# A hybrid decoder layer on one core: k and the second half's x transposed by VectorE blocks and transfers, two sample products run in pairs

## The chip, the cores and the metric

The kernel runs on one core of a Trainium2 chip. The core has TensorE (PE, with its weight loads shown as PEld), VectorE (DVE), ScalarE (ACT), GpSimd (POOL) and SyncE (SP), which issues all DMAs of this kernel on one queue in program order. The metric is the device time of one launch in microseconds (us); lower is better.

## The reference, cut to what matters

One layer (depth 1) is applied to a prompt of 2048 tokens and to a sample group of 8 sequences with 4 tokens each, with the same weights; the width is 1024 and there are 8 heads of 128.

```python
h = _layernorm(x) * (1 + scale) + shift          # scale, shift from silu(c) @ w_ada
p = h @ w_in                                     # 9232 columns
u_a, v_a, z_a, qkv, z_b, b_raw, a_raw, ga, gb = split(p)
y_a = gelu(u_a) * (tril(w_s) @ layernorm(gelu(v_a)) + b_s) * silu(z_a)   # chunks of 128 tokens
q, k, v = silu(causal depthwise conv of width 4 over qkv)
q, k = l2norm per head; beta = sigmoid(b_raw); g = -exp(a_log) * softplus(a_raw + dt_bias)
# gated delta rule, chunked:  S_t = a_t S_(t-1) + beta_t k_t (v_t - a_t S_(t-1)^T k_t)^T,  o_t = S_t^T q_t
y_b = rmsnorm(o) * silu(z_b)
m = sigmoid(ga) * (y_a @ w_pa) + sigmoid(gb) * (y_b @ w_pb)
x_new = layernorm(ALPHA * x + gate * (m @ w_o))
```

For the sample group the delta rule starts from a given state of 8 sequences x 8 heads x 128 x 128, and the new states are outputs too.

## The kernel before

The prompt is worked on in two halves of 1024 tokens; the sample's 32 tokens ride with the first half. Each half runs the same list of column groups ("groups") of 128 output columns: for each head k, q, v, z_b and (heads 0 to 5) g_a, then g_b, v_a, u_a with z_a, the rest of g_a, then the products with w_pa, w_pb and w_o. A group is computed in column pieces of tokens, `CG`: 384, 384 and 256+32 tokens in the first half, 512 and 512 in the second. Every fp32 operand is split into two fp32r parts, so one piece is 8 x 3 matmuls into one of three PSUM banks (role `mm`), and its "sink" (a generator such as `qkv_sink`) then evacuates the bank.

All activations live transposed (features on partitions, tokens along the row), so whatever needs tokens on partitions is transposed. `k_token` does that for k with TensorE (`tp`, one 128x128 transpose for each chunk of 128 tokens), takes the squares' sums from PSUM on ACT, and writes the scaled k into the buffer `KV`, which `chain` reads. `q_token` transposes q the same way, for the norm alone. `v_token` has another route: `qkv_sink` transposes v in 32x32 blocks on VectorE (`vtrans`), and four DMAs write the blocks to DRAM (`d_v`) in runs of 32 elements so that a fifth DMA reads them back with tokens on partitions. The convolution's working buffers have the role `cp`: there are two, taken for each sink of k, q and v; k and q give theirs back when the product with the tanh has been written to `KQ`, v gives its back after the fourth write to `d_v`.

`gram` of a head needs q and k of a piece and the norm of k (`cc`, made in `k_token`). `inverse` follows `gram`, and `chain` walks the 8 chunks of a half in order. When the last head of the second half is done (`headdone`), the Y buffers take the split weights of v_a (`v_take`), and `v_tokens` multiplies with them. While the first half's later groups run, `h_next` normalizes x of the second half, transposes it by `tp` (8 chunks x 8), applies scale and shift out of PSUM (`affine`) and writes it to `d_h`; `h_tiles` loads it back at the end of the first half and splits it.

`sample_head` does the sample's delta rule for one head: eight products `kx` (64 output columns, 128 columns streamed) accumulate q and k against the eight sequences' states, and two products with `kp` (32 rows contracted, 512 columns streamed) make the update of the states.

The order of instructions on every engine is fixed when the program is built: a list scheduler (`Sched`) takes the steps of all generators, gives each step an assumed duration and lets the step that can start first go next. On the chip the engines follow that order and wait on semaphores.

Of the kernel before, what the change touches and what calls it, by code (L numbers as in the profile page):

```python
# [169 lines left out]
def hybrid_step_kernel(ctx: ExitStack, tc: tile.TileContext, x_prompt, x_sample, state_conv, state_ssm,  # L170
# [53 lines left out]
    def dram(name, n):  # L224
        return dr_pool.tile([1, n], F32, name=name)[:]
# [6 lines left out]
    def role(name, cands):  # L232
        roles[name] = cands
# [8 lines left out]
    def Yc(first, n):  # L242
        return (YO + first * UNIT, xs_units(32, first, n))
# [95 lines left out]
    def SCR(**kw):  # L339
# [18 lines left out]

    d_v = {(half, h, i): dram(f"d_v{half}{h}{i}", n * P)
           for half, ns in enumerate(((384, 384, 256), (512, 512))) for h in range(H) for i, n in enumerate(ns)}  # L360

# [439 lines left out]
    def h_next(c):  # L801

        yield from x_norm(1, c, "hb")
        xb, t0 = S.ev[("xn", 1, c)]
        e = 0.0
        for i in range(2):
            pb = yield ("a", "pt")
            t = t0
            for k in range(4):
                t = yield from tp(Q(pb[0], k * P, P), V(xb[0] + (4 * i + k) * P, P), dep=max(t, pb[2]))  # L810
            fb = yield ("a", "hf")
            tg = max(t, fb[2])
            for k in range(4):
                t = yield from affine(V(fb[0] + k * P, P), Q(pb[0], k * P, P), 4 * i + k, k < 2, tg)
                e = max(e, t)
            S.release(pb, e)
            t = yield from dma(DV(d_h, 4 * i * P * HALF + c * P, [HALF, P], [P * HALF, 4], [1, P]),
                               V(fb[0], [P, 4], [1, P]), dep=e)
            S.release(fb, t)
            S.signal(("hB", c, i), t + 500)  # L820
        S.release(xb, e)

    def h_next_all():
        for c in range(8):
            S.spawn(h_next(c), 2.0)
            if c:
                yield ("w", ("hB", c - 1, 1))

# [7 lines left out]
    def h_tiles(todo, role, after):  # L836
        if after is not None:
            yield ("w", after)
        while todo:
# [6 lines left out]
            for c in range(8):  # L846
                t = max(t, (yield ("w", ("hB", c, k // 4))))
# [339 lines left out]
    def qkv_sink(half, s, h):  # L1187
# [13 lines left out]
        def sink(cgi, pb, t):  # L1201
# [38 lines left out]
            else:  # L1240
# [11 lines left out]
                S.spawn(k_token(half, h, cgi, t) if s == 1 else q_token(half, h, cgi, t), 1)  # L1252
            if ns_:
# [57 lines left out]

    def k_token(half, h, cgi, t):
        me = hd(half, h)
        tk = yield ("w", ("kd", half, h))
        cs = chunks(half, cgi)
        m, c0 = len(cs), cs[0]
        hs = me["hs"][0]
        if "KV" not in me:
            if "KVw" not in me:
                me["KVw"] = True  # L1320
                kv = yield ("a", "KV")
                me["KV"] = kv
                S.signal(("KV", half, h), kv[2])
        ta = yield ("w", ("KV", half, h))
        pb = yield ("a", "pt")
# [14 lines left out]
        S.release(pb, t)  # L1340
# [303 lines left out]
    def sample_head(h):  # L1644
        me = hd(0, h)
        t = 0.0
        for s in range(3):
# [25 lines left out]
        t = yield from pow_(V(o_vf, 1, **k32), V(o_vf, 1, **k32), 1)  # L1673
        kp, vs = x + 64, x + 192
        t = yield from ts(V(kp, P, **k32), Q(pb[0], 0, P, **k32), V(o_kf, 1, **k32), ALU.mult)
        t = yield from ts(V(vs, P, **k32), Q(pb[0], P, P, **k32), V(o_vf, 1, **k32), ALU.mult)
        S.release(pb, t)
        es, npq, am, m2, us = x + 320, x + 352, x + 416, x + 448, x + 480
        t1 = yield from tt(V(es, NS, **k32), V(gr, NS, **k32), V(c_mns, NS, **k32), ALU.add, dep=t1)
# [8 lines left out]
        t = yield from tp(Q(pb[0], 64, NS, **k32), V(npq, NS, **k32))  # L1688
        t = yield from act(V(am, NS, **k32), Q(pb[0], 64, NS, **k32))
# [3 lines left out]
        t = yield from tt(V(us, NS, **k32), V(m2, NS, **k32), Q(pb[0], 128, NS, **k32), ALU.subtract)  # L1693
        S.release(pb, t)
# [10 lines left out]
        t4 = 0.0  # L1705
# [4 lines left out]
        rb = yield ("a", "Rb")  # L1710
        t = yield from stt(V(rb[0], P, **k32), Q(pb[0], 0, P, **k32), V(c_sneg + h, 1, **k32), V(vs, P, **k32),
                           ALU.mult, ALU.add, dep=max(t4, t, rb[2]))
        osb = yield ("a", "Xb")
        q32 = dict(p0=32, np_=32)
        t5 = yield from act(V(osb[0], P, **q32), Q(pb[0], 0, P, **q32), dep=max(t4, osb[2]))
        S.release(pb, max(t, t5))
        pb = yield ("a", "pt")
        t = yield from mm(Q(pb[0], 0, P, **k32), V(us, NS, **k32), V(rb[0], P, **k32), dep=max(t, pb[2]))
        t = yield from act(V(rb[0], P, **k32), Q(pb[0], 0, P, **k32))
        tx = t  # L1720
# [12 lines left out]
        tz = yield ("w", ("zz", 0, h, len(CG[0]) - 1))  # L1733
        ys = x + 448
        t = yield from stt(V(ys, NS), Q(pb[0], 0, NS), V(c_ong, 1), V(me["ZZ"][0] + HALF, NS),
# [7 lines left out]
                           bc(V(egr + 3, [4, 8]).unsqueeze(2), [P, 8, P]), ALU.mult, dep=max(t2, t4))  # L1743
        for i in range(2):
            xe = yield ("a", "kx")
            t1 = yield from tt(V(xe[0], [P, 4], [1, P], **k32), bc(V(rb[0], P, **k32).unsqueeze(1), [NS, 4, P]),
                               bc(V(c_sel + 4 * i, 4, **k32).unsqueeze(2), [NS, 4, P]), ALU.mult, dep=max(tx, xe[2]))
            pb = yield ("a", "pt")
            t = yield from mm(Q(pb[0], 0, 512), V(kp, P, **k32), V(xe[0], 512, **k32), dep=max(t1, pb[2]))
            S.release(xe, t)  # L1750
            a = V(sb0[0] + 512 * i, 512)
            t = yield from tt(a, a, Q(pb[0], 0, 512), ALU.add, dep=max(t, t2))
            S.release(pb, t)
        S.release(rb, t1)
# [561 lines left out]
```

## Time and profile before

| what | value |
|---|---|
| runs | 2719.08, 2723.06, 2724.36 us (median 2723.06) |
| the profiled execution | 2721.62 us, of which the span from the first to the last instruction is 2719.9 us |
| PE / PEld busy | 2676.6 us (98%) / 2351.3 us (86%) |
| DVE / ACT / POOL busy | 1467.0 us (54%) / 1002.8 us (37%) / 557.0 us (20%) |
| mean granted TensorE clock | 0.997 |
| DMA queue | 445402 packets, 269.89 MB, 34.6% of 16 engines' span |

Times in the rows below are in microseconds from the span's start unless a row says ns. An fp32 matmul shows as two records, a transpose or an fp32r matmul as one. A record's duration includes the pipeline's latency, so what one costs is read from start to start.

### The profile page before, as it was taken

The page shows a single profiled execution, that of the slowest core. Times are in us where ns is not written, and L with a number is a line of the kernel's source. Part 1 is how long each engine was busy: PE and PEld are TensorE (multiplying, and loading weights), DVE is VectorE, ACT ScalarE, POOL GpSimd, SP SyncE. Part 2 cuts the span into 40 slices and gives each one's busy share as a digit, 9 for nine tenths or more (in the row PEclk, how much of TensorE's full clock was granted, in tenths as well). Part 3 has the DMA queues.
Part 4 walks back from the last instruction along what each step waited for, and adds up shares of the span by engine and source line. Part 5 has one row for each costly group of instructions (what it writes and reads, how often), then busy time and mean ns, then how long its engine had stood idle before and what let it go on. Part 6 is the DMA issues. An engine that isn't in the chain of part 4 may idle for free.

```text
span 2719.9 us, 44021 instructions
## 1 busy us (share of the span) xinstructions
PE 2676.6 (98%) x16386; PEld 2351.3 (86%) x16386; DVE 1467.0 (54%) x3234; ACT 1002.8 (37%) x2710; POOL 557.0 (20%) x1452
## 2 busy tenths in 40 slices
PE   6999999999999999999999999999999999999998
PEld 3989999999899999999997888888888888888876
DVE  5677667777652353433547666666662323433446
ACT  5544444545343222221224535344542312222120
POOL 2044544324400000000000443433351000000001
PEclk9999999999999999999999999999999999999999
DMA  6232333223463232332433333333332422233332
GB/s 214 68 95 78 90 105 91 72 70 101 141 211 95 64 115 76 94 105 91 140 109 101 96 97 81 85 93 78 84 86 83 125 99 76 72 112 104 108 121 85
DMA packets 445618, 272.70 MB, mean 100 GB/s; under 512 B 141530, under 2 KB 411154, under 8 KB 445403
## 3 DMA queue, kind: packets, MB, share of 16 engines
q1 hardware_dynamic: 445402, 269.89, 34.6%
q8 instruction: 128, 2.10, 0.3%
q14 instruction: 88, 0.71, 0.1%
HBM read 205.70 MB, written 64.10 MB: 99 GB/s over the span
## 4 chain that ended last, share of the span: by engine, by line
PE 95%; DMA 2%; DVE 1%; ACT 1%; issue 0%; SPq 0%; POOL 0%; POOLq 0%; ACTq 0%; DVEq 0%
PE psum L447 90%; PE psum L452 3%; DMA arena<-in_w_o_dram 0%; ACT arena L398 0%; DMA arena<-in_w_in_dram 0%; PE psum L1483 0%; PE psum L1509 0%; PE psum L1520 0%; DVE arena L730 0%; DMA arena<-in_state_ssm_dram 0%; DVE arena L732 0%; PE psum L1489 0%; DVE arena L423 0%; PE psum L650 0%; DMA Y0F<-in_x_prompt_dram 0%
## 5 line engine op out<-in xcount | busy, mean ns | idle before, releaser
L447 PE MATMUL psum<-TX,TWHL 128*128 128x384 f32 (+3 forms) x9296 | 1973.4, 360 | 3.8 <-DVE TX L407 3.4
L447 PEld LDWEIGHTS psum<-TX,TWHL 128*128 128x128 f32 (+1 forms) x9296 | 1554.6, 188 | 164.0 <-issue 10.6
L398 ACT ACTIVATE arena<-psum 128x128 bf16<-128x128 f32 (+10 forms) x920 | 311.8, 348 | 769.9 <-PE psum L447 587.9
L436 POOL TENSOR_TENSOR arena<-arena 128x4 f32<-128x4 f32 (+4 forms) x139 | 120.1, 865 | 1598.3 <-DVE arena L417 1388.7
L423 DVE SCALAR_TENSOR_TENSOR arena<-arena 128x512 f32<-128x512 f32 (+8 forms) x625 | 345.8, 563 | 95.3 <-ACT arena L398 84.9
L410 POOL TENSOR_TENSOR arena<-arena 128x60 f32<-128x60 f32 (+24 forms) x992 | 358.6, 361 | 169.6 <-DMA d_v<-arena 57.5
L407 DVE TENSOR_TENSOR TWHL<-arena,TWHL 128x512 fp32r<-128x512 f32 (+1 forms) x344 | 233.1, 685 | 240.9 <-ACT TWHL L398 238.7
L423 DVE SCALAR_TENSOR_TENSOR arena<-arena,psum 128x128 f32<-128x128 f32 (+3 forms) x342 | 132.2, 403 | 360.3 <-PE psum L447 249.9
L398 ACT ACTIVATE TWHL<-arena 128x512 fp32r<-128x512 f32 x344 | 214.3, 627 | 219.1 <-PE psum L447 103.4
L398 ACT ACTIVATE arena<-arena 128x128 f32<-128x128 f32 (+9 forms) x509 | 229.4, 486 | 118.2 <-DVE arena L423 81.8
L407 DVE TENSOR_TENSOR arena<-arena 128x1024 f32<-128x1024 f32 (+13 forms) x259 | 114.3, 446 | 15.0 <-DMA arena<-in_lnv_g_dram 4.9
L447 PE MATMUL psum<-arena 128*128 128x128 f32 (+8 forms) x524 | 102.3, 293 | 1.2 <-ACT arena L398 1.0
L452 PE MATMUL psum<-arena 128*128 128x128 f32 (+7 forms) x381 | 93.2, 269 | 3.4 <-ACT TX L398 1.5
L423 DVE SCALAR_TENSOR_TENSOR arena<-psum,arena 128x512 f32<-128x512 f32 (+4 forms) x80 | 39.8, 509 | 103.8 <-PE psum L447 103.8
L447 PEld LDWEIGHTS psum<-arena 128*128 128x128 f32 (+5 forms) x524 | 73.7, 162 | 22.9 <-issue 11.2
L1228 POOL COPY arena<-arena 128x3 f32<-128x3 f32 x120 | 34.7, 289 | 267.7 <-ACT arena L398 266.8
L398 ACT ACTIVATE TX<-arena 128x512 fp32r<-128x512 f32 (+2 forms) x84 | 47.3, 587 | 93.6 <-DMA arena<-d_yb 74.2
L398 ACT ACTIVATE Y7F<-psum 32x256 f32<-32x256 f32 (+6 forms) x115 | 46.6, 405 | 86.0 <-PE psum L447 38.4
L398 ACT ACTIVATION_READ_ACCUMULATOR arena<-psum 128x1 f32 x392 | 76.6, 195 | 0.0
L452 PEld LDWEIGHTS psum<-arena 128*128 128x128 f32 (+7 forms) x381 | 49.9, 136 | 23.0 <-issue 11.9
L407 DVE TENSOR_TENSOR TX<-arena,TX 128x512 fp32r<-128x512 f32 (+2 forms) x84 | 52.4, 639 | 26.3 <-ACT TX L398 25.7
L417 DVE TENSOR_SCALAR arena<-arena 128x3 f32<-128x3 f32 (+10 forms) x234 | 47.8, 209 | 34.0 <-ACT arena L398 25.8
(244 smaller groups left out, 2733.6 us busy)
## 6 DMA issues: line engine op xcount, KB each, us to landing
arena<-in_w_in_dram SPq DMA_DIRECT2D x288, 256.0 KB
out_dram<-arena SPq DMA_DIRECT2D x25, 512.0 KB
arena<-in_x_prompt_dram SPq DMA_DIRECT2D x24, 512.0 KB
arena<-d_gc SPq DMA_DIRECT2D x16, 512.0 KB
arena<-d_blk SPq DMA_DIRECT2D x64, 128.0 KB
d_yb<-arena SPq DMA_DIRECT2D x32, 256.0 KB
d_vh<-arena SPq DMA_DIRECT2D x16, 512.0 KB
arena<-d_vh SPq DMA_DIRECT2D x16, 512.0 KB
```

The costliest lines, as they stand in the source:

```text
L398: nc.scalar.activation(out, in_, func, **kw)
L407: nc.vector.tensor_tensor(out=out, in0=a, in1=b, op=op)
L410: nc.gpsimd.tensor_tensor(out=out, in0=a, in1=b, op=op)
L417: nc.vector.tensor_scalar(out=out, in0=a, scalar1=s1, scalar2=s2, op0=op0, **kw)
L423: nc.vector.scalar_tensor_tensor(out=out, in0=a, scalar=s, in1=b, op0=op0, op1=op1)
L436: nc.gpsimd.tensor_tensor(out=out, in0=a, in1=e, op=ALU.pow)
L447: nc.tensor.matmul(out, lhsT, rhs, start=start, stop=stop)
L452: nc.tensor.transpose(out, in_, ident[: in_.shape[0], : in_.shape[0]] if idn is None else idn)
L1228: nc.gpsimd.tensor_copy(V(c_tail + gi, [24, 3]), V(x0 + n0, 3))
```

## The change

- `k_token` no longer uses TensorE. `qkv_sink` transposes k in blocks on VectorE, and a new `tokens` does for k what `v_token` does for v: four writes to a new DRAM buffer `d_k`, one load into `KV`. The squares and the scaling then read `KV`. The `cp` buffer of a k sink is given back after the fourth write.
- `h_next` transposes a whole chunk of x by one VectorE instruction and writes it with four DMAs in runs of 32 elements; scale and shift move to `h_tiles`, where they are applied to a loaded tile of 128x1024.
- In `sample_head` the eight `kx` products go to two column halves of the array in turn, each half accumulating in its own 64 partitions; an ACT copy and a VectorE addition join them. The two `kp` products go to two groups of 32 rows, with copies of `kp` and of the right operand on partitions 32 to 63.

```diff
-    role("hf", [Yc(2, 1), Yc(3, 1), Yc(6, 1), Yc(7, 1)])
+    role("hf", [Yc(2, 2), Yc(6, 2)])
...
     def h_next(c):
         yield from x_norm(1, c, "hb")
-            for k in range(4):
-                t = yield from tp(Q(pb[0], k * P, P), V(xb[0] + (4 * i + k) * P, P), dep=max(t, pb[2]))
...
-                t = yield from affine(V(fb[0] + k * P, P), Q(pb[0], k * P, P), 4 * i + k, k < 2, tg)
...
+        fb = yield ("a", "hf")
+        t = yield from vtrans(V(fb[0], D), V(xb[0], D), dep=max(t, fb[2]))
+        S.release(xb, t)
+        for i in range(4):
+            t = yield from dma(DV(d_h, c * P + 32 * i, [HALF, 32], [32 * HALF, 32], [1, 32]),
+                               V(fb[0], [32, 32], [1, 32], p0=32 * i, np_=32), dep=t)
...
             t = yield from dma(V(b[0], HALF), DV(d_h, k * P * HALF, [HALF, P], [1, HALF]), dep=max(t, b[2]))
+            t = yield from affine(V(b[0], HALF), V(b[0], HALF), k, k % 2 == 0, t)
             t = max(t, (yield ("w", ("Xfree", 1, k))))
...
                 t = yield from stt(dst, V(x0, n0), 1.0, y, ALU.add, ALU.mult, dep=max(t, ta))
-                S.release(xb, t)
                 S.signal(("kq", half, h, s, cgi), t)
+                if s == 1:
+                    t = yield from vtrans(V(x0, n0), dst)
+                    S.spawn(k_token(half, h, cgi, xb, t), 1)
+                else:
+                    S.release(xb, t)
+                    S.spawn(q_token(half, h, cgi, t), 1)
...
+    def tokens(src, dst, d, m, t, key):
+        for i in range(4):
+            t = yield from dma(DV(d, 32 * i, [P, 32], [32 * P, 4 * m], [1, 32]),
+                               V(src[0], [32, 4 * m], [1, 32], p0=32 * i, np_=32), dep=t)
+        S.release(src, t)
+        t = max(t, (yield ("w", key)))
+        return (yield from dma(dst(), DV(d, 0, [P, P], [P * P, m], [1, P]), dep=t))
+
+    def k_token(half, h, cgi, xb, t):
...
-        pb = yield ("a", "pt")
-        for i, c in enumerate(cs):
-            t = yield from tp(Q(pb[0], i * P, P), V(me["KQ"][0] + c * P, P), dep=max(t, pb[2]))
+        t = yield from tokens(xb, lambda: V(me["KV"][0] + c0 * P, [P, m], [1, P]), d_k[half, h, cgi], m, t,
+                              ("KV", half, h))
...
-            t = yield from act(SCR(), Q(pb[0], i * P, P), AF.Square, accum=V(hs + 16 + c, 1), dep=te)
+            t = yield from act(SCR(), V(me["KV"][0] + c * P, P), AF.Square, accum=V(hs + 16 + c, 1), dep=max(te, tk))
...
-        t = yield from tt(V(me["KV"][0] + c0 * P, [P, m], [1, P]), Q(pb[0], 0, [P, m], [1, P]),
-                          bc(kf.unsqueeze(2), [P, m, P]), ALU.mult, dep=max(t, ta))
+        t = yield from tt(kv, kv, bc(kf.unsqueeze(2), [P, m, P]), ALU.mult, dep=t)
...
-            t4 = yield from mm(Q(pb[0], 0, P, np_=64), V(kx + 64 * b, 64), V(sb0[0] + b * P, P),
-                               start=b == 0, stop=b == NB - 1, dep=max(t3, td, pb[2]))
+            nc.tensor.matmul(Q(pb[0], 0, P, p0=64 * (b % 2), np_=64), V(kx + 64 * b, 64), V(sb0[0] + b * P, P),
+                             start=b < 2, stop=b >= NB - 2)
...
+        t4 = yield from act(o64, Q(pb[0], 0, P, p0=64, np_=64), dep=max(t4, osb[2]))
+        t4 = yield from tt(o64, Q(pb[0], 0, P, np_=64), o64, ALU.add)
...
-            t = yield from mm(Q(pb[0], 0, 512), V(kp, P, **k32), V(xe[0], 512, **k32), dep=max(t1, pb[2]))
+        for i, q in enumerate((pb, pc)):
+            rows = dict(p0=32 * i, np_=32)
+            nc.tensor.matmul(Q(q[0], 0, 512), V(kp, P, **rows), V(xe[0], 512, **rows), start=True, stop=True)
```

## Rows read from the trace of the kernel before

**Rows 1.** The page: busy time of the engines, and shares of the chain by engine.
```profile
PE 2676.6 (98%) x16386; PEld 2351.3 (86%) x16386; DVE 1467.0 (54%) x3234; ACT 1002.8 (37%) x2710; POOL 557.0 (20%) x1452
...
PE 95%; DMA 2%; DVE 1%; ACT 1%; issue 0%; SPq 0%; POOL 0%; POOLq 0%; ACTq 0%; DVEq 0%
```

**Rows 2.** Windows, all but the first 60 us: PE, PEld, DVE, ACT, POOL busy, clock, DMA share.
```profile
60.00:2720.00 2660.00, 2641.47 (x16173) 2331.41 (x16171) 1432.95 (x3134) 965.47 (x2647) 541.59 (x1403) 1.00 0.34 97
```

**Rows 3.** Groups by line and shape, PE: transposes that read Y0 and Y1.
```profile
L452 PE MATMUL psum<-arena,Y0F 128*128 128x128 f32 x176 | 44.3, 275 | 0.8 <-ACT Y0F L398 0.8
...
L452 PE MATMUL psum<-arena,Y1F 128*128 128x128 f32 x144 | 39.1, 276 | 0.4 <-DVE Y1F L423 0.4
```

**Rows 4.** Timeline of PE: start, time to the end, instruction; two transposes in succession.
```profile
767.52 0.27 PE L452 MATMUL psum<-arena 128*128 128x128 f32 x1
767.63 0.27 PE L452 MATMUL psum<-arena,Y0F 128*128 128x128 f32 x1
```

**Rows 5.** Timeline of PE around the eight `kx` products of one head.
```profile
304.88 1.56 PE L447 MATMUL psum<-TX,TWHL 128*128 128x384 f32 x8
306.37 1.96 PE L447 MATMUL psum<-arena 128*64 128x128 f32 x16
308.26 2.02 PE L447 MATMUL psum<-TX,TWHL 128*128 128x384 f32 x10
```

**Rows 6.** Timeline of PE around one of the two `kp` products of one head.
```profile
238.61 1.39 PE L447 MATMUL psum<-TX,TWHL 128*128 128x384 f32 x7
239.93 1.12 PE L447 MATMUL psum<-arena 32*128 32x512 f32 x2
240.98 0.45 PE L447 MATMUL psum<-TX,TWHL 128*128 128x384 f32 x1
```

**Rows 7.** Timeline of PE in `inverse`: two quarters of the array.
```profile
200.69 0.22 PE L1520 MATMUL psum<-Y7F 64*64 64x64 f32 x1
200.69 0.22 PE L1522 MATMUL psum<-Y7F 64*64 64x64 f32 x1
```

**Rows 8.** The tile `d_v`: SP's issue times (ns), and who waited.
```profile
L381 SPq DMA_DIRECT2D d_v<-arena x160: 302/459/1661, 109.0 to 2023.7; - x160
...
  DVE Y5F L407: 1.5, 3
```

**Rows 9.** Timeline of DVE: a v piece transposed, then used after its return.
```profile
523.09 0.57 DVE L429 STREAM_TRANSPOSE arena<-arena 128x384 f32<-128x384 f32 x1
...
540.64 0.56 DVE L407 TENSOR_TENSOR Y5F<-Y5F,arena 128x384 f32<-128x384 f32 x1
```

**Rows 10.** Timeline of POOL: first copies into `cp` for k0, k2, v0, v2 and next k0.
```profile
476.71 0.19 POOL L1210 COPY arena<-arena 128x3 f32<-128x3 f32 x1
...
486.24 0.45 POOL L1210 COPY arena<-arena 128x3 f32<-128x3 f32 x1 [2.00 <-DVE Y1F L423]
...
510.92 0.19 POOL L1210 COPY arena<-arena 128x3 f32<-128x3 f32 x1 [1.15 <-DVE Y1F L423]
...
536.68 0.19 POOL L1210 COPY arena<-arena 128x3 f32<-128x3 f32 x1
555.26 0.18 POOL L1210 COPY arena<-arena 128x3 f32<-128x3 f32 x1
```

**Rows 11.** Timeline of DVE, last head of the second half: last k and q.
```profile
1986.69 0.74 DVE L423 SCALAR_TENSOR_TENSOR Y1F<-arena 128x512 f32<-128x512 f32 x1 [1.53 <-ACT arena L398]
...
2001.40 0.68 DVE L423 SCALAR_TENSOR_TENSOR Y1F<-arena 128x512 f32<-128x512 f32 x1
```

**Rows 12.** Timelines of DVE and PE: last split that `v_tokens` needs, its first matmul.
```profile
2130.02 0.29 DVE L407 TENSOR_TENSOR Y7R<-arena,Y7R 128x128 fp32r<-128x128 f32 x1
...
2133.57 0.86 PE L447 MATMUL psum<-Y0R,TX 128*128 128x512 f32 x3
```

**Rows 13.** Timeline of PE at the second half's first matmuls.
```profile
1461.34 1.07 PE L447 MATMUL psum<-TX,TWHL 128*40 128x512 f32 x2 [2.55 <-DVE TX L407]
```

**Rows 14.** Groups by line and shape, DVE: scale or shift of 1024 columns in SBUF.
```profile
L417 DVE TENSOR_SCALAR arena<-arena 128x1024 f32<-128x1024 f32 x16 | 12.9, 805 | 5.7 <-POOL arena L436 5.7
```

More of the change, by code (lines that the diff above doesn't have):

```diff
@@ L357, in hybrid_step_kernel @@
     d_td = [dram(f"d_td{i}", 32 * 1024) for i in range(2)]
-    d_v = {(half, h, i): dram(f"d_v{half}{h}{i}", n * P)
-           for half, ns in enumerate(((384, 384, 256), (512, 512))) for h in range(H) for i, n in enumerate(ns)}
+    d_v, d_k = ({(half, h, i): dram(f"d_{x}{half}{h}{i}", n * P)
+                 for half, ns in enumerate(((384, 384, 256), (512, 512))) for h in range(H) for i, n in enumerate(ns)}
+                for x in "vk")
     def fsz(ap):
@@ L531, in init_small, with init_sel @@
         S.signal("small", t)
+    def init_sel():
+        t = yield ("w", ("ada", 0))
+        yield from ts(V(c_sel, 4, p0=32, np_=32), V(c_sel + 4, 4, np_=NS), 1.0, ALU.mult, dep=t)
     def init_vec():
@@ L803, in h_next @@
         yield from x_norm(1, c, "hb")
-        xb, t0 = S.ev[("xn", 1, c)]
-        e = 0.0
-        for i in range(2):
-            pb = yield ("a", "pt")
-            t = t0
-            for k in range(4):
-                t = yield from tp(Q(pb[0], k * P, P), V(xb[0] + (4 * i + k) * P, P), dep=max(t, pb[2]))
-            fb = yield ("a", "hf")
-            tg = max(t, fb[2])
-            for k in range(4):
-                t = yield from affine(V(fb[0] + k * P, P), Q(pb[0], k * P, P), 4 * i + k, k < 2, tg)
[L815 to L821, printed above, removed]
+        xb, t = S.ev[("xn", 1, c)]
+        fb = yield ("a", "hf")
[4 more added lines that the diff above has]
+                               V(fb[0], [32, 32], [1, 32], p0=32 * i, np_=32), dep=t)
+        S.release(fb, t)
+        S.signal(("hB", c), t + 500)
     def h_next_all():
@@ L826, in h_next_all @@
             if c:
-                yield ("w", ("hB", c - 1, 1))
+                yield ("w", ("hB", c - 1))
     def h_load():
@@ L846, in h_tiles @@
             for c in range(8):
-                t = max(t, (yield ("w", ("hB", c, k // 4))))
+                t = max(t, (yield ("w", ("hB", c))))
             t = yield from dma(V(b[0], HALF), DV(d_h, k * P * HALF, [HALF, P], [1, HALF]), dep=max(t, b[2]))
+            t = yield from affine(V(b[0], HALF), V(b[0], HALF), k, k % 2 == 0, t)
             t = max(t, (yield ("w", ("Xfree", 1, k))))
@@ L1320, in k_token @@
                 me["KVw"] = True
[L1321 to L1325, printed above, removed]
-        for i, c in enumerate(cs):
-            t = yield from tp(Q(pb[0], i * P, P), V(me["KQ"][0] + c * P, P), dep=max(t, pb[2]))
+                S.spawn(kv_take(half, h), 0.95)
+        t = yield from tokens(xb, lambda: V(me["KV"][0] + c0 * P, [P, m], [1, P]), d_k[half, h, cgi], m, t,
+                              ("KV", half, h))
+        tk = yield ("w", ("kd", half, h))
+        hs = me["hs"][0]
+        kv = V(me["KV"][0] + c0 * P, [P, m], [1, P])
         te = t
         for i, c in enumerate(cs):
-            t = yield from act(SCR(), Q(pb[0], i * P, P), AF.Square, accum=V(hs + 16 + c, 1), dep=te)
+            t = yield from act(SCR(), V(me["KV"][0] + c * P, P), AF.Square, accum=V(hs + 16 + c, 1), dep=max(te, tk))
         nk, cc, kf, vf = (V(hs + 16 + 8 * i + c0, m) for i in range(4))
@@ L1344, in k_token, with kv_take @@
         S.signal(("vf", half, h, cgi), t)
+    def kv_take(half, h):
+        me = hd(half, h)
+        me["KV"] = yield ("a", "KV")
+        S.signal(("KV", half, h), me["KV"][2])
     def v_token(half, h, cgi, yb, t):
@@ L1675, in sample_head @@
         t = yield from ts(V(kp, P, **k32), Q(pb[0], 0, P, **k32), V(o_kf, 1, **k32), ALU.mult)
+        t = yield from ts(V(kp, P, p0=32, np_=32), V(kp, P, **k32), 1.0, ALU.mult, dep=t)
         t = yield from ts(V(vs, P, **k32), Q(pb[0], P, P, **k32), V(o_vf, 1, **k32), ALU.mult)
         S.release(pb, t)
-        es, npq, am, m2, us = x + 320, x + 352, x + 416, x + 448, x + 480
+        es, npq, am, m2, us = x + 320, x + 352, x, x + 320, x + 416
         t1 = yield from tt(V(es, NS, **k32), V(gr, NS, **k32), V(c_mns, NS, **k32), ALU.add, dep=t1)
@@ L1688, in sample_head @@
         t = yield from tp(Q(pb[0], 64, NS, **k32), V(npq, NS, **k32))
-        t = yield from act(V(am, NS, **k32), Q(pb[0], 64, NS, **k32))
+        t = yield from act(V(am, NS, **k32), Q(pb[0], 64, NS, **k32), dep=max(t, t2))
         t = yield from mm(Q(pb[0], 96, NS, **k32), V(am, NS, **k32), V(npq, NS, **k32))
@@ L1692, in sample_head @@
         t = yield from mm(Q(pb[0], 128, NS, **k32), V(am, NS, **k32), V(m2, NS, **k32))
-        t = yield from tt(V(us, NS, **k32), V(m2, NS, **k32), Q(pb[0], 128, NS, **k32), ALU.subtract)
+        t = yield from tt(V(us, [NS, 2], [1, NS], **k32), bc(V(m2, NS, **k32).unsqueeze(1), [NS, 2, NS]),
+                          bc(Q(pb[0], 128, NS, **k32).unsqueeze(1), [NS, 2, NS]), ALU.subtract)
         S.release(pb, t)
@@ L1733, in sample_head @@
         tz = yield ("w", ("zz", 0, h, len(CG[0]) - 1))
-        ys = x + 448
+        ys = x + 320
         t = yield from stt(V(ys, NS), Q(pb[0], 0, NS), V(c_ong, 1), V(me["ZZ"][0] + HALF, NS),
@@ L1743, in sample_head @@
                            bc(V(egr + 3, [4, 8]).unsqueeze(2), [P, 8, P]), ALU.mult, dep=max(t2, t4))
[L1744 to L1748, printed above, removed]
-            t = yield from mm(Q(pb[0], 0, 512), V(kp, P, **k32), V(xe[0], 512, **k32), dep=max(t1, pb[2]))
-            S.release(xe, t)
+        xe = yield ("a", "kx")
+        t1 = yield from tt(V(xe[0], [P, 4], [1, P], np_=64), bc(V(rb[0], P, np_=64).unsqueeze(1), [64, 4, P]),
+                           bc(V(c_sel, 4, np_=64).unsqueeze(2), [64, 4, P]), ALU.mult, dep=max(tx, xe[2]))
+        pb = yield ("a", "pt")
+        pc = yield ("a", "pu")
+        t = yield ("o", "PE", 900.0, max(t1, pb[2], pc[2]))
+        for i, q in enumerate((pb, pc)):
+            rows = dict(p0=32 * i, np_=32)
+            nc.tensor.matmul(Q(q[0], 0, 512), V(kp, P, **rows), V(xe[0], 512, **rows), start=True, stop=True)
+        S.release(xe, t)
+        te = t
+        for i, q in enumerate((pb, pc)):
             a = V(sb0[0] + 512 * i, 512)
-            t = yield from tt(a, a, Q(pb[0], 0, 512), ALU.add, dep=max(t, t2))
-            S.release(pb, t)
+            t = yield from tt(a, a, Q(q[0], 0, 512), ALU.add, dep=max(te, t2))
+            S.release(q, t)
         S.release(rb, t1)
@@ L2269, in hybrid_step_kernel @@
         S.spawn(init_vec(), 1.015)
+        S.spawn(init_sel(), 1.6)
         start()
```

22 lines of the change are left out of this document (9 added, 13 removed).

## The prediction

> **What bounds the kernel now.** I read the page first: PE is busy for 2676.6 of 2719.9 us, and the chain that ended last consists of PE for 95% [rows 1]. The windows then say where the missing 43.3 us are: after the first 60 us PE is idle for only 2660.00 - 2641.47 = 18.5 us, at a granted clock of 1.00 [rows 2]. The reader is to see that DVE at 54%, ACT and the DMAs have room on average, and that almost any work taken off PE should shorten the run, unless something new makes PE wait. So I price PE's instructions from start to start, then look for waits that the change could create where a result is already used soon after it is made.
>
> **What is removed from PE.**
>
> *Transposes.* The rows of Y0 and Y1 hold 176 + 144 = 320 transposes [rows 3]; by the code these are 128 of k, 128 of q (which stay) and 64 of x. So 192 go. Two transposes in succession start 767.63 - 767.52 = 0.11 us apart [rows 4], though each record lasts 0.27. That is 192 x 0.11 = 21.1 us.
>
> *The `kx` products.* From 304.88 to 308.26 there are 3.38 us with 8 projection matmuls and the 16 records of eight products [rows 5]. A projection matmul of 384 columns costs 0.17 (8 of them take 1.56 us [rows 5], 7 take 1.39 [rows 6]), so the 16 records cost 3.38 - 8 x 0.17 = 2.0 us, entry and exit included. Each streams 128 columns and I take the 0.11 of [rows 4] for it. Two halves of the array side by side leave 8 such steps: 8 x 0.11 = 0.88 saved per head, 7.0 us for 8 heads.
>
> *The `kp` products.* From 238.61 to 240.98 there are 2.37 us with 7 projection matmuls (1.19) and one product: 1.18 us [rows 6]. There are two in each head, apart from each other; side by side they cost about one: 8 x 1.18 = 9.4 us.
>
> That parts of the array work at the same time is seen in `inverse`: two products in different quarters both start at 200.69 [rows 7]. There both rows and columns differ. No row shows two groups of rows alone that write all columns, so the 9.4 has 0 as its lower bound, and the 7.0 as well if the halves did not overlap; I take the full values because [rows 7] is the nearest case. The Trainium skill ("TensorE: Matmul & The Clock Gate", Part 3, Measured speedup vs the span model) has a price where no row here has one: four groups of 32 rows with 512 columns ran 3.07 times as fast as in succession. An estimate from that page, 3.07/4 of my 9.4, is 7.2, and the sum would be 2.2 us smaller.
>
> Sum: 21.1 + 7.0 + 9.4 = 37.5 us off PE. Nothing substantial is added to it (one product of the sample gets 64 instead of 32 stationary columns).
>
> **What is added elsewhere.** DVE: 40 block transposes of k, like the 40 of v, at about 0.57 for 384 columns [rows 9], some 24 us; eight of x with 1024 columns, bounded below by 0.57 and above by 3 x 0.57, some 10 us. The scale and shift in `h_tiles` are eight instructions, four on ACT and four on DVE, 0.8 each on DVE [rows 14], in place of 64 small ones. With DVE at 54% [rows 1] this is covered by PE's work, and it would cost at most its own 37 us if it were not. SP issues 160 + 40 more DMAs for k and 16 for x, at the 0.46 us of a write of `d_v` [rows 8] about 100 us, spread over 2700.
>
> In four places the work is late next.
>
> *(a) `cp`.* A k sink keeps its buffer until its fourth write has landed. SP's queue is also passed by weight loads: they are issued ahead, and v's writes stand among them today without PE idling. Below I cost the buffer: with today's rows k0's comes round after 486.24 - 476.71 = 9.5 us, v0's after 536.68 - 510.92 = 25.8, in a head of 555.26 - 476.71 = 78.6 [rows 10]. The wait for the second k0 ended by the product that frees it. PE has three banks, so a sink that is late by up to two pieces does not stop it. Bounds: nothing, or the slower rival below. I take 3 us.
>
> *(b) `gram` of the last head.* The path of v takes 540.64 - 523.09 = 17.5 us from the start of the transpose to the use [rows 9]. With that, and about 3 us for squares and norm, the norm of the last k piece is ready at 1986.69 + 0.74 + 20.5 = 2008; today the last piece of q lets `gram` go at 2001.40 + 0.68 = 2002 [rows 11]. `inverse`, `chain` and the Y buffers follow one another and shift by the same 6 us. Their last consumer has a margin of 2133.57 - (2130.02 + 0.29) = 3.3 us [rows 12]. So PE would wait for about 3 us there. For the other heads, the shift is a latency behind which other groups run. Bounds: 0 and 6.
>
> *(c) The second half's start.* PE already waits 2.55 us for the last splits of x [rows 13]; they now come after one more instruction of 0.8 us for each tile [rows 14], two of which follow each other at the end. I take 1.5 us, bounds 0.8 and 3.
>
> *(d)* Squares on ACT and the scaling on DVE now wait for a load, with all that stands behind them in those queues: PSUM evacuations, for which PE waits. The same kind of wait behind v's load took 1.5 us in the whole run, in 3 cases [rows 8], so I put it at nothing; if it were as bad as one write for each of the 40 loads, 40 x 0.46 = 18 us.
>
> **The sum.** 37.5 - 3 - 3 - 1.5 = 30 us. The profiled execution took 2721.6 (2719.9 and 1.7 around it), which gives 2691.6. The median of the runs shown is 1.4 above that execution, so I predict 2693.
>
> **The rivals.**
>
> *The pairs do not overlap* (the change doesn't do what it says for them). Then 7.0 and 9.4 stay on PE: 2693 + 16.4 = 2709. For it: no row shows rows-only pairs [rows 7]. Against: the two starts at the same time. 10%.
>
> *The `cp` buffers delay PE part of the time.* In the first half nine sinks in succession ask for two buffers. If k0 to k2 hold them like v, the queue of waiting sinks is longer than two pieces for some of them. With 2 to 3 us lost per head in 8 heads it is 2693 + 20 = 2713. For it: v2 takes its buffer as late as 25.8 us after v0 [rows 10]. Against: PE idles nowhere in that stretch now, v2's delay included [rows 2]. 20%.
>
> *Slower: `cp` becomes the bound.* If each k and v piece really needs 25.8 us and each q piece 9.5 [rows 10], a head of the first half needs (3 x 25.8 + 3 x 9.5 + 3 x 25.8) / 2 = 91.6 us on two buffers, against 78.6 now: 13 us more for each of 7 periods. It decides as soon as the six long holds exceed (2 x 78.6 - 28.5) / 6 = 21.4 us; from there each further microsecond costs 3 per head or 21 in 7 periods, while what is gained outside these heads is 64 transposes of x and 64 of k in the second half, 128 x 0.11 = 14. At 22.1 us the run is as long as before, at 23 it is 2723 + 1.6 x 21 - 14 = 2743. For it: the hold of v in [rows 10]. Against: 25.8 is the time until the next one took the buffer, waiting for data included; the block transpose of that v0 began at 523.09 [rows 9], 12.2 us after its buffer was taken, and a sink that has waited for its buffer has its data ready and needs less. The Trainium skill ("DMA: Bandwidth & Descriptors", Rules for kernel authors) speaks for this rival: to transpose it wants the hardware's DMA transpose and not a plain DMA with a rearranged access pattern, 19 times slower. By that rule the four writes would be the long part of each hold. The rows of v, which does it this way, bound the whole way out and back to 17.5 us [rows 9], so I don't scale anything by 19. 10%.
>
> *No measurable difference:* gain and waits cancel within 0.2% (5.4 us, about what the scatter of the three runs lets one tell). 5%.
>
> **How the numbers follow.** The forecast, 2680 to 2703 (waits between 0 and 13 us, pairs whole), has 55%. Faster by over 0.2%: 55 + 10 + 20 = 85%. Same: 5%. Slower: 10%. For 8 in 10 the range goes from 2680 (all of 37.5 and a little from fewer changes of array layout) to 2717, which takes in the two rivals that halve the gain.
>
> **What would show it.** In the profile after: 128 rows fewer of each kind among transposes of Y0 and Y1, leaving 128; PE busy near 2640; records of `kx` and `kp` starting in pairs a few ns apart; idle of PE still near 18 us after the first 60, with up to 3 more at the start of `v_tokens` and at the second half's start. Wrong would be: the second row of a `kp` pair half a microsecond behind the first; PE idle in the heads of the first half before projections, ended by an evacuation whose buffer waited for a write of `d_k`; ACT waiting on loads of `d_k` for tens of microseconds.

## The result, and the profile after

The changed kernel takes 2760.0 us (median of 4 runs, 2757.0 to 2763.2) against 2722.1 for the kernel before (4 runs on the same chip): the ratio is 1.0139, 95% interval 1.0123 to 1.0155. It is slower by 38 us; 30 less were forecast, with a range that ended at 2717.

The page of the changed kernel, busy time by engine and the chain by engine, to be read against [rows 1]:

```profile
PE 2670.9 (97%) x16194; PEld 2354.9 (85%) x16194; DVE 1488.6 (54%) x3263; ACT 1001.7 (36%) x2682; POOL 566.1 (21%) x1452
...
PE 89%; DMA 3%; DVE 2%; POOL 2%; ACT 2%; issue 1%; SPq 1%; POOLq 0%; ACTq 0%; DVEq 0%
```

Its windows, with columns as in [rows 2] (width, PE, PEld, DVE, ACT and POOL busy, granted clock, DMA share, GB/s):

```profile
60.00:2758.50 2698.50, 2634.85 (x15980) 2334.16 (x15978) 1454.26 (x3162) 964.37 (x2618) 551.09 (x1403) 0.98 0.37 102
60.00:200.00 140.00, 124.41 (x806) 114.51 (x805) 86.19 (x238) 68.69 (x213) 40.72 (x108) 0.91 0.31 76
200.00:800.00 600.00, 578.02 (x4273) 537.29 (x4272) 408.43 (x1058) 267.39 (x897) 230.82 (x629) 0.95 0.42 105
800.00:1400.00 600.00, 600.00 (x3750) 586.57 (x3750) 248.84 (x474) 169.85 (x342) 11.99 (x17) 1.00 0.39 113
```

After the first 60 us PE is idle for 2698.5 - 2634.85 = 63.7 us, where it was 18.5 [rows 2]. Of these, 15.6 + 22.0 = 37.6 lie between 60 and 800 us, in the heads of the first half, and there the clock column shows 0.91 and 0.95 where it was 1.00. PE's busy time hardly fell, 2676.6 to 2670.9, although 192 instructions have gone: the rest of the work ran partly at a granted clock of 1.2 instead of 2.4 GHz.

The work that was to go from PE has gone. Groups by line and shape of the changed kernel, the transposes that answer to [rows 3]:

```profile
L453 PE MATMUL psum<-arena,Y1F 128*128 128x128 f32 x64 | 18.1, 283 | 0.0
L453 PE MATMUL psum<-arena,Y0F 128*128 128x128 f32 x64 | 17.2, 279 | 1.2 <-DVE Y0F L424 1.2
```

PE's timeline of the changed kernel around one head's two `kp` products, and then around one head's `kx` products [rows 6, 5]:

```profile
202.36 1.13 PE L1771 MATMUL psum<-arena 32*128 32x512 f32 x4
203.41 0.49 PE L448 MATMUL psum<-arena,Y7F 128*128 128x128 f32 x2
...
243.29 0.86 PE L448 MATMUL psum<-TX,TWHL 128*128 128x384 f32 x4
244.09 1.09 PE L1722 MATMUL psum<-arena 128*64 128x128 f32 x16
245.11 0.79 PE L448 MATMUL psum<-TX,TWHL 128*128 128x384 f32 x3
```

128 transposes are left. The 16 records of `kx` take 245.11 - 243.29 - 4 x 0.17 = 1.1 us instead of 2.0, and both `kp` products together 203.41 - 202.36 = 1.05 instead of 2 x 1.18.

What PE waits for now (the changed kernel's waits by releaser: us in total, times, longest):

```profile
PE psum L448 <- ACT arena L399: 19.0, 14, 3.9
...
PE psum L1493 <- DVE arena L1469: 7.0, 5, 3.0
...
PE psum L448 <- DVE TX L408: 6.5, 3, 4.9
...
PE psum L448 <- ACT Y0R L399: 4.7, 1, 4.7
```

The same view for POOL, whose copy at L1207 is the first into a newly taken `cp` buffer (L1210 before; there, no such row named a write of k):

```profile
POOL arena L1207 <- DMA d_k<-arena: 100.7, 18, 11.2
```

One case, in head 3 of the first half: the timeline of the changed kernel, of which the block transposes of the pieces k1 and k2 and the rows of SP from 340 us on are shown, and the three at the end that follow from them.

```profile
339.56 0.57 DVE L430 STREAM_TRANSPOSE arena<-Y1F 128x384 f32<-128x384 f32 x1
...
340.26 0.82 SPq L382 DMA_DIRECT2D d_k<-arena  x2
...
341.18 2.92 SPq L382 DMA_DIRECT2D d_td<-arena  x4
...
344.15 0.60 SPq L382 DMA_DIRECT2D d_k<-arena  x1
...
344.86 0.41 SPq L382 DMA_DIRECT2D Y5F<-d_k  x1
...
345.53 0.38 SPq L382 DMA_DIRECT2D arena<-d_td  x1
...
345.95 0.57 SPq L382 DMA_DIRECT2D d_k<-arena  x1
...
346.57 1.04 SPq L382 DMA_DIRECT2D arena<-in_w_in_dram  x2
...
349.88 0.45 DVE L430 STREAM_TRANSPOSE arena<-Y1F 128x256 f32<-128x256 f32 x1
...
350.41 1.34 SPq L382 DMA_DIRECT2D d_k<-arena  x3
...
353.64 0.49 ACT L399 ACTIVATE arena<-psum 128x384 f32<-128x384 f32 x1 [1.18 <-DMA d_k<-arena]
...
353.72 0.19 POOL L1207 COPY arena<-arena 128x3 f32<-128x3 f32 x1 [10.08 <-DMA d_k<-arena]
...
354.19 0.69 PE L448 MATMUL psum<-TX,TWHL 128*128 128x384 f32 x1 [2.78 <-ACT arena L399]
```

Piece k1 is transposed by 339.56 + 0.57 = 340.13, and its first write is the first of the two at 340.26; the second is k0's fourth, which stands behind it in the queue. Before k1's second, third and fourth, SP issues writes and a load of `inverse` (`d_td`), the load of k0 and two of weights, each in its place in the queue. The fourth is the second of the three at 350.41. The first of them is k2's first write, which the program issues ahead of it, so SP, done with the weights at 346.57 + 1.04 = 347.61, stands still until k2's block transpose has ended at 349.88 + 0.45 = 350.33. So k1's buffer comes free only when k2 has been transposed. In each of the heads 1 to 7 of the first half the program issues k0's fourth write behind k1's first, in heads 3 and 7 k1's behind k2's as well. k1's fourth has landed when POOL and ACT go on at 353.6, ACT evacuates the next projection into the buffer, and PE gets its PSUM bank back after 2.78 us. Four issues that need 1.9 us by themselves (4 x 0.47, the median of the 160) stretch over 10.

In this wait of PE, and in one of 0.50 us at 343.0, the ACT instruction that ended it had itself waited for a write of `d_k`. The other waits in the heads were not followed back so far; that they come with the hold is shown by the experiments.

The period of one head shows the same. POOL's timeline of the changed kernel, the copies for k0, k2, v0, v2 and the next k0 in head 5, as in [rows 10]:

```profile
494.51 0.19 POOL L1207 COPY arena<-arena 128x3 f32<-128x3 f32 x1
...
518.65 0.19 POOL L1207 COPY arena<-arena 128x3 f32<-128x3 f32 x1 [6.08 <-DMA d_k<-arena]
...
540.18 0.58 POOL L1207 COPY arena<-arena 128x3 f32<-128x3 f32 x1 [2.69 <-DVE Y1F L424]
...
561.38 0.18 POOL L1207 COPY arena<-arena 128x3 f32<-128x3 f32 x1
579.89 0.19 POOL L1207 COPY arena<-arena 128x3 f32<-128x3 f32 x1
```

k0's buffer comes round after 24.1 us instead of 9.5, the nine sinks take 66.9 us to v2 instead of 60.0, and the period is 85.4 instead of 78.6.

### The profile page after: what moved, and what is told of

Same layout as the page of the kernel before. It is cut to its first block, busy times and chain, and to the rows that moved or that the text cites. A ratio compares the mean times of both kernels' runs of the same rounds, so it can differ in the third digit from the quotient of the medians.

```text
span 2758.5 us, 44131 instructions
## 1 busy us (share of the span) xinstructions
PE 2670.9 (97%) x16194; PEld 2354.9 (85%) x16194; DVE 1488.6 (54%) x3263; ACT 1001.7 (36%) x2682; POOL 566.1 (21%) x1452
## 4 chain that ended last, share of the span: by engine, by line
PE 89%; DMA 3%; DVE 2%; POOL 2%; ACT 2%; issue 1%; SPq 1%; POOLq 0%; ACTq 0%; DVEq 0%
PE psum L448 85%; PE psum L453 2%; POOL arena L411 2%; ACT arena L399 1%; DVE arena L424 1%; SPq L382 1%; DVE arena L408 0%; DMA arena<-d_gc 0%; PE psum L1530 0%; PE psum L1519 0%; DMA d_v<-arena 0%; PE psum L1771 0%; PE psum L1493 0%; DMA arena<-in_w_in_dram 0%; DMA Y1F<-in_w_ada_dram 0%
## 5 line engine op out<-in xcount | busy, mean ns | idle before, releaser
L448 PEld LDWEIGHTS psum<-TX,TWHL 128*128 128x128 f32 (+1 forms) x9296 | 1573.9, 190 | 183.0 <-ACT arena L399 19.6
L399 ACT ACTIVATE arena<-psum 128x128 bf16<-128x128 f32 (+10 forms) x792 | 275.3, 359 | 743.5 <-PE psum L448 573.9
L437 POOL TENSOR_TENSOR arena<-arena 128x4 f32<-128x4 f32 (+4 forms) x139 | 130.0, 936 | 1599.3 <-DVE arena L418 1389.8
L424 DVE SCALAR_TENSOR_TENSOR arena<-arena 128x512 f32<-128x512 f32 (+9 forms) x633 | 348.9, 561 | 75.3 <-ACT arena L399 63.4
L408 DVE TENSOR_TENSOR arena<-arena 128x4 f32<-128x4 f32 (+12 forms) x251 | 108.1, 436 | 17.8 <-DMA arena<-d_gc 7.0
L1207 POOL COPY arena<-arena 128x3 f32<-128x3 f32 x120 | 34.8, 290 | 264.7 <-DMA d_k<-arena 100.7
L418 DVE TENSOR_SCALAR arena<-arena 128x3 f32<-128x3 f32 (+7 forms) x247 | 52.6, 218 | 44.0 <-ACT arena L399 33.8
L448 PEld LDWEIGHTS psum<-arena 128*128 128x128 f32 (+3 forms) x364 | 55.9, 171 | 21.9 <-issue 7.5
L448 PE MATMUL psum<-arena 128*128 128x128 f32 (+5 forms) x364 | 67.8, 270 | 5.8 <-DVE arena L408 4.5
L453 PEld LDWEIGHTS psum<-arena 128*128 128x128 f32 (+8 forms) x381 | 49.6, 136 | 22.8 <-issue 10.3
L1225 POOL COPY arena<-arena 128x3 f32<-128x3 f32 x120 | 32.5, 272 | 142.9 <-ACT arena L399 141.8
```

Source lines behind the costliest of these rows:

```text
L399: nc.scalar.activation(out, in_, func, **kw)
L408: nc.vector.tensor_tensor(out=out, in0=a, in1=b, op=op)
L418: nc.vector.tensor_scalar(out=out, in0=a, scalar1=s1, scalar2=s2, op0=op0, **kw)
L424: nc.vector.scalar_tensor_tensor(out=out, in0=a, scalar=s, in1=b, op0=op0, op1=op1)
L437: nc.gpsimd.tensor_tensor(out=out, in0=a, in1=e, op=ALU.pow)
L448: nc.tensor.matmul(out, lhsT, rhs, start=start, stop=stop)
```

## The experiments

The theory to be tested, H: the hold of `cp` by k's four writes is the loss. Its rivals: L, ACT and DVE stand behind the loads of `d_k`; P, the longer chain of the sample with its pairs; and x.

**e1, k by PE.** The change without its part on k.

```
-                    t = yield from vtrans(V(x0, n0), dst)
-                    S.spawn(k_token(half, h, cgi, xb, t), 1)
+                S.release(xb, t)
+                S.spawn(k_token(half, h, cgi, t) if s == 1 else q_token(half, h, cgi, t), 1)
...
+            t = yield from tp(Q(pb[0], i * P, P), V(me["KQ"][0] + c * P, P), dep=max(t, pb[2]))
```

> k is transposed by PE again (as before the change); x by VectorE and the pairs stay. Theory H (hold: a k piece keeps its cp buffer until four writes have left SP's queue, the next projection can't be evacuated, PE waits and its clock falls) and theory L (load: ACT and DVE stand behind loads of d_k and PE waits for them) both say that the loss is in k: before minus 7.0 for x minus 16.4 for the pairs plus 2 at the start of the second half, 2695 to 2710 us. Theory P (the sample's chain with its pairs is longer, PE waits in its fixed order): 2745 or more.

Measured: 2693.9 us, ratio 0.9901 (0.9886 to 0.9916), a microsecond under the range. The loss is in k; P falls.

**e2, block transpose into KV.** The same writes and loads, only from another place.

```
-                    t = yield from vtrans(V(x0, n0), dst)
-                    S.spawn(k_token(half, h, cgi, xb, t), 1)
+                    tv = yield ("w", ("KV", half, h))
+                    t = yield from vtrans(V(me["KV"][0] + c0, n0), dst, dep=max(t, tv))
+                    S.release(xb, t)
+                    S.spawn(k_token(half, h, cgi, (me["KV"][0] + c0,), t), 1)
...
-        S.release(src, t)
```

> As the changed kernel, but k's block transpose writes into the KV buffer where the load later puts k, and the four writes are made from there; cp comes free behind the block transpose, as for q. Number and order of transfers, loads, squares: as in the changed kernel. Theory H: 2690 to 2705 us, POOL's copies at the start of the sinks no longer wait for writes of d_k. Theory L: 2745 to 2765 us, since ACT and DVE wait for the same loads. Theory P: 2745 to 2765.

Measured: 2694.3 us, ratio 0.9903 (0.9886 to 0.9919), 66 below the changed kernel: as H has it and not as L. But the waits that L speaks of went too: ACT waits for loads of `d_k` for 20.1 us in 9 cases in the changed kernel and for 0.5 us in one here. So e2 by itself doesn't tell the hold from the loads; e6 says more. Windows of e2, with the sum over the span:

```profile
60.00:800.00 740.00, 735.89 (x5451) 683.97 (x5452) 517.85 (x1347) 357.27 (x1158) 277.36 (x743) 1.00 0.46 116
...
sum 2689.30, PE 2638.10 PEld 2327.85 DVE 1486.01 ACT 996.13 POOL 567.90; mean PE 527.62 PEld 465.57 DVE 297.20 ACT 199.23 POOL 113.58
```

What PE still waits for in e2, the rows behind the first 60 us that are above 3 us:

```profile
PE psum L448 <- DVE TX L408: 6.5, 3, 4.8
...
PE psum L448 <- ACT Y0R L399: 4.9, 1, 4.9
```

Between 60 and 800 us PE is idle for 4.1 us and the clock is back at 1.00. The spans of the changed kernel and of e2 differ by 2758.5 - 2689.3 = 69.2 us; idle time makes (2758.5 - 2670.9) - (2689.3 - 2638.1) = 36.4 of them, and the same matmuls at a lower clock 2670.9 - 2638.1 = 32.8. By POOL's copies for k0 the changed kernel loses 15.0 us against e2 in head 0 (its period is 143.3 - 52.1 = 91.2, e2's 127.5 - 51.3 = 76.2) and 5.6 in the mean in the six after it (662.4 - 143.3 against 613.2 - 127.5).

**e3, no pairs; e4, x by PE.** Each undoes one of the other parts; the lines are those of the change, taken back.

> The sample's products as before the change; k and x by VectorE and transfers. Theories H and L: 16.4 us of PE's work come back, 2770 to 2785 us. Theory P: the waits go, 2705 to 2730 us.

> The second half's x is transposed by PE again; k and the pairs as in the changed kernel. By the sum, 64 transposes of 0.11 us come back and the longer wait at the start of the second half goes: +7.0 - 2.3 = +5, so 2765 us (2758 to 2772) by theories H, L and P alike. If x were the loss, 2720 to 2740.

Measured: 2772.6 us (1.0183, 1.0160 to 1.0207) and 2764.0 (1.0155, 1.0140 to 1.0170). They lie 12.6 and 4.0 above the changed kernel: neither part is the loss. The pairs are a gain even there, near the forecast; the 4.0 for x lie within the intervals.

**e6, one write.** Is it the number of transfers or the time to the last write? k stays in `cp`, but leaves it as it lies in one write, and the rearranging is done by four loads.

```
-        for i in range(4):
-            t = yield from dma(DV(d, 32 * i, [P, 32], [32 * P, 4 * m], [1, 32]), ...
+        t = yield from dma(DV(d, 0, [m * P, P], [1, m * P]), V(src[0], m * P), dep=t)
         S.release(src, t)
...
-        return (yield from dma(dst(), DV(d, 0, [P, P], [P * P, m], [1, P]), dep=t))
+        for i in range(4):
+            t = yield from dma(dst(i), DV(d, 32 * i, [m * P, 32], [P, m], [32 * m * P, 4], [1, 32]), dep=tw)
```

> As the changed kernel (k's block transpose stays in the cp buffer), but k leaves it in one write as it lies, and four loads bring it back in order. cp comes free when one write has landed and not the fourth of four, which stands 6 to 7 us behind the first in SP's queue. The number of transfers is the same. Theory H: most of the loss goes, 2695 to 2725 us. If the number of transfers in SP's queue, or the time until k is back, were the loss: 2750 or more.

Measured: 2691.7 us, ratio 0.9887 (0.9872 to 0.9901), at or below the lower end of what H gave. POOL's row in the waits of e6:

```profile
POOL arena L1207 <- DMA d_k<-arena: 86.0, 18, 10.3
```

POOL still waits for k's write as often and nearly as long as in the changed kernel (100.7), and nothing is lost: this row alone would have misled. What differs is when the buffer comes free, and whether PE by then needs the bank. Over the 24 k pieces of the first half, from POOL's copy to 2 us (the landing) behind the issue of the last write, a hold lasts 18.6 us in the mean in the changed kernel and 11.9 here; before, to the end of the multiplication that frees it, it was 10.9. (q held 9.5 and v 20.5 in the changed kernel.) ACT waits for loads of `d_k` for 10.8 us in 8 cases here, about half of what it was, and this costs nothing that shows.

Each of these kernels has its own order of instructions, since `Sched` plans it anew, and an order alone can be worth some microseconds (e11 below). That three different ways of ending the hold early (e1, e2, e6) come within 3 us of one another, 66 to 68 below the changed kernel, speaks against an accident of the order.

**e7, v from KV too.** As e2, with v's block transpose written to its place in KV in the same way.

> As e2, and v's block transpose goes to KV as well, so that no cp buffer waits for a write. In e2 POOL waits for writes of d_v in cp for 8.9 us only, and PE for none of it: 2691 to 2696 us, no difference from e2. If v's hold still cost something there: 2680 to 2688.

Measured: 2695.1 us, ratio 0.9898 (0.9882 to 0.9914): no difference from e2. The hold of `cp` is no longer what limits.

**e5, the last head.** As e2, with k by PE in one head of sixteen.

```
+                if s == 1 and (half, h) == (1, H - 1):
+                    S.release(xb, t)
+                    S.spawn(k_token_pe(half, h, cgi, t), 1)
```

> As e2 (k's block transpose goes to KV), but in the last head of the second half k is transposed by PE, so that its gram, inverse and chain start earlier. In e2 PE waits 4.9 us at the start of v_tokens and the clock is low for 6.8 us behind it. If that is the late chain of the last head, as step (b) of the prediction has it: 2694.3 - 4.9 - 3.4 + 8 x 0.11 = 2687 us. If the wait has another cause: 2693 to 2697.

Measured: 2695.1 us, ratio 0.9895 (0.9878 to 0.9911). So it is not the late chain of the last head: the wait is still there (4.71 us). PE's timeline of the kernel before, from the last transpose of the last head's chain to `v_tokens`, begins to say what it is:

```profile
2111.07 0.27 PE L452 MATMUL psum<-arena 128*128 128x128 f32 x1
2111.09 22.64 PE L447 MATMUL psum<-TX,TWHL 128*128 128x512 f32 x96
2133.57 0.63 PE L447 MATMUL psum<-Y0R,TX 128*128 128x512 f32 x2
```

The same stretch in e2, whose timeline has the same rows as that of e5:

```profile
2084.71 0.27 PE L453 MATMUL psum<-arena 128*128 128x128 f32 x1
2084.74 11.45 PE L448 MATMUL psum<-TX,TWHL 128*128 128x512 f32 x48
2101.07 1.65 PE L448 MATMUL psum<-Y0R,TX 128*128 128x512 f32 x3 [4.89 <-ACT Y0R L399]
```

Between the chain's end and the splits that `v_tokens` needs PE used to have 96 matmuls of another projection, 22.5 us; now 48 of them have been done earlier, and 11.4 us are too short.

**e11, k by PE in the second half.** Does that follow from the 64 transposes taken off PE in this half?

```
+                if s == 1 and half == 1:
+                    S.release(xb, t)
+                    S.spawn(k_token_pe(half, h, cgi, t), 1)
```

> As e6 (k leaves cp in one write) in the first half, k transposed by PE in the second half. Theory F: at the end of the second half's heads the chain of the last head decides and not PE's work, so that 64 transposes taken off PE there only let PE run out of the projections that fill this chain, and it waits 4.5 to 4.9 us at the start of v_tokens with a low clock behind it. Then this wait goes here, and the time stays within 3 us of e6's 2691.7. If PE's work decided there: + 64 x 0.08 to 0.11 = 5 to 7 us, 2697 to 2699.

Measured: 2698.8 us, ratio 0.9902 (0.9888 to 0.9917). The median is 7 us above e6's, where the rival put it and F did not; but the two ran on different chips, and against the kernel before on each the difference is 4 us, with intervals that overlap. PE's timeline of e11 in the same stretch:

```profile
2087.72 22.64 PE L448 MATMUL psum<-TX,TWHL 128*128 128x512 f32 x96
2110.20 0.86 PE L448 MATMUL psum<-Y0R,TX 128*128 128x512 f32 x3
```

The 96 matmuls are back and the wait is gone, as F has it. From the wait at the second half's start (1434.0 us; e6: 1429.0) to the end of the span (2696.6; 2690.1) it takes 1.5 us more than e6; the other 5 arise in the first half, where the code is the same but the order that `Sched` wrote is not (one wait of 2.63 us at 336). So the 64 transposes were worth about 1.5 us in that half by these two executions; the medians alone don't show it, and it stays open how much of it is the order.

**e9, pairs alone; e10, x alone.** The kernel before with one part of the change.

> The kernel before with only the sample's products in pairs. By the prediction's terms 7.0 + 9.4 = 16.4 us less on PE: 2722 - 16 = 2706 us (2702 to 2710). If they are hidden behind something else, or the longer chain of the sample makes PE wait: 2715 or more.

> The kernel before with only the second half's x transposed by VectorE. By the prediction's terms 64 transposes of 0.11 us less and 1.5 us more wait at the second half's start: 2722 - 5.5 = 2716.5 us (2713 to 2720). e1, which has x and the pairs, came out at 2693.9, which is 28 below before; with 16 for the pairs x would be worth 12: 2710.

Measured: 2703.1 us, ratio 0.9919 (0.9903 to 0.9936), and 2713.8, ratio 0.9963 (0.9948 to 0.9978), against 2725.4 for before on that chip: 22 and 12 us gained, 6 more each than the terms, with intervals of 4 to 5 us to either side. These parts do at least what they were forecast to do; where the rest is from was not tried.

**e8, stalls.** What does an idle stretch of PE cost? Into the kernel before, between 800 and 1400 us where PE hardly ever waits:

```
+            nc.tensor.transpose(Q(pb[0], 0, 32, np_=32), V(c_ident, 32, np_=32), ident[:32, :32])
+            nc.scalar.activation(a, Q(pb[0], 0, 32, np_=32), AF.Copy)
+            for _ in range(k):
+                nc.gpsimd.tensor_tensor(out=a, in0=a, in1=V(c_ident, 32, np_=32), op=ALU.mult)
+            nc.tensor.transpose(Q(pb[0], 64, 32, np_=32), a, ident[:32, :32])
```

> The kernel before with twelve short stalls put into PE's order in the middle stretch where PE never waits: a transpose on PE, a copy on ACT, 1, 2, 4, 6, 8 or 10 small products on POOL (twice each) and a transpose that needs them. The output doesn't change. By an estimate from 0.6 us of hand-over and 0.31 a product the stalls sum to 26 us. Theory I (an idle stretch of PE costs its own length): 2748 us. Theory C (behind the longer ones the clock is granted at 1.2 GHz for a while, as behind the 2.55 us at the second half's start of the kernel before, where 6.8 us ran at half the clock): some 8 times 1.7 to 3.4 more, 2762 to 2775 us.

Measured: 2764.2 us, ratio 1.0152 (1.0137 to 1.0167), 41.9 more. What PE waited for the stalls, from the waits of e8:

```profile
PE psum L2273 <- POOL arena L2272: 25.6, 12, 3.5
```

Windows of e8 around the eight stalls of 1.6 us and more; the clock is the third column from the right:

```profile
962.00:975.00 13.00, 11.01 (x61) 10.74 (x60) 5.72 (x8) 2.61 (x6) 1.34 (x4) 0.87 0.71 200
1010.00:1030.00 20.00, 17.47 (x111) 16.78 (x110) 8.59 (x17) 3.67 (x8) 1.45 (x6) 1.00 0.24 65
1060.00:1080.00 20.00, 17.11 (x104) 16.79 (x103) 5.25 (x9) 4.13 (x9) 1.93 (x8) 0.91 0.11 27
1110.00:1125.00 15.00, 11.46 (x64) 11.06 (x63) 2.81 (x6) 2.83 (x8) 2.42 (x10) 0.89 0.22 65
1253.00:1270.00 17.00, 15.38 (x94) 14.99 (x94) 2.77 (x5) 1.45 (x3) 0.97 (x4) 1.00 0.27 77
1301.00:1311.00 10.00, 6.91 (x26) 6.49 (x25) 2.33 (x4) 1.24 (x3) 2.28 (x6) 0.66 0.13 45
1352.00:1362.00 10.00, 6.70 (x25) 6.28 (x24) 2.87 (x5) 1.87 (x4) 2.33 (x8) 0.66 0.23 77
1403.00:1414.00 11.00, 7.46 (x31) 6.75 (x30) 3.06 (x10) 3.36 (x7) 2.42 (x10) 0.69 0.47 144
```

Width times what the clock lacks of 1.00 sums to 1.7 + 1.8 + 1.7 + 3.4 + 3.4 + 3.4 = 15.4 us; with the 25.6 that is 41.0 of the 41.9, as theory C has it.

## Why the prediction was wrong, step by step

*Work off PE, 37.5 us:* right in size. In e2, which has all three parts, PE's busy time is 2676.6 - 2638.1 = 38.5 us less, and the pairs overlap fully.

*Step (a), `cp`, 3 us:* this is the step that failed. It was worth 2760.0 - 2694.3 = 66 us, by e2 and e6. The hold by four writes was seen, and the slower rival named the place and the sign, but its point of decision was wrong: it let the long holds spread over the whole period of a head, (2 x 78.6 - 28.5) / 6 = 21.4 us. The nine sinks come in one stretch, though, 60 of the 78.6 us [rows 10], and the rest of the period gives nothing back. With the holds of the changed kernel the rival's own formula gives (3 x 18.6 + 3 x 9.5 + 3 x 20.5) / 2 = 72.9 us, less than 78.6 and so no loss; against e2 the loss was 5.6 us per head, and 15 in the first. "SP's queue is also passed by weight loads" was read as harmless: each of the four writes waits for whatever the queue has in front of it, the next piece's first write and its block transpose among them, and the buffer waits for the last of the four. That v's writes stand there "today without PE idling" was so, but the view of [rows 8] has a row that was not shown, by which a copy into `cp` already waited 6.0 us for a write of v:

```profile
  POOL arena L1210: 6.0, 1
```

*The price of PE's waits* was their length alone, here as in the rival of 2713. Nearly as much again, 32.8 beside 36.4 us, went to work at the lower clock behind them. [rows 2] had no example in the heads, but the 2.55 us of [rows 13] could have been looked at for it.

*Step (b), `gram` of the last head, 3 us:* the size was near (4.9 us of wait, and a lower clock behind it), the cause was not. e5 takes the longer way of k out of the last head and the wait stays; PE arrives earlier, with less other work left to cover the same chain.

*Step (c), the second half's start, 1.5 us:* 4.86 - 2.55 = 2.3 us, within its bounds.

*Step (d), loads of `d_k`, nothing:* ACT waited 20.1 us for them, in 9 cases, in the changed kernel, more than the 18 of the step's upper bound, though not all that ACT waits reaches PE; in e6 10.8 are left and nothing is lost. They were not tried apart from the hold, so a part of the 66 us may have come by way of them. The 1.5 us in 3 cases from which the step put them at nothing were DVE's waits for one of the two `KV` buffers alone; the other adds 1.1 us in 2 cases.

So the sum of 2691.6 was that of a kernel in which k doesn't hold `cp` longer: e2 and e6 came out at 2694.3 and 2691.7. That it fits so well is in part luck. The pairs and x have 16.4 + 5.5 = 21.9 us in the sum and gained 27.0 together in e1; k has 14.1 for its 128 transposes, less 3 each for (a) and (b), 8.1 in all, and e6 is 2.2 us below e1. The two errors nearly cancel. The rule of the Trainium skill that was set against the change ("DMA: Bandwidth & Descriptors", Rules for kernel authors) pointed the right way, but not by its reason: e6 still rearranges by plain transfers and loses nothing.

Of the three parts only two are shown to pay. With k left to PE (e1) the kernel takes 2693.9, with k by transfers at its best 2691.7, too near to tell apart. e2 has 10.3 us less busy time on PE than e1 (2648.4 - 2638.1) and 7.4 more idle (51.2 against 43.8), above all before `v_tokens`.

## What to carry to other kernels

Before a result goes out by transfers, ask which buffer it leaves from, how many of those there are, and what stands in the queue before the last of the writes and is itself still waiting there; if the result is written once as it lies and rearranged on the way back, or written from the place where it will end up, the buffer is free sooner. Compare holds with the stretch in which the buffers are asked for, not with the period. And where PE sets the time, ask whether a wait of it will cost more than its length.

## What the runs showed of the hardware that was not expected

A wait of PE can cost more than itself. In e8, 25.6 us in twelve stalls cost 41.9. Of the eight stalls of 1.6 us or more, six were followed by a stretch at 1.2 GHz, though PE had work at once; those of 2.5 us (near 1012) and 1.6 us (near 1254) were not, one of 2.0 us (near 962) was. In the changed kernel two `kp` products came 2.07 us late at 604.8, and the clock stayed low while further waits followed (windows: 15 us, of which PE was busy for 13.1, at 0.54):

```profile
604.00:619.00 15.00, 13.07 (x143) 10.35 (x144) 8.65 (x21) 4.43 (x17) 0.71 (x4) 0.54 0.49 120
```
